# mLSTM gate preparation turned by VectorE and DMA, begun in the second token-major group; its loads and those of the heads two steps ahead of use

## The chip, the cores and the metric

The kernel runs on 1 core of one Trainium2 chip. The metric is the device time of one execution in microseconds. Before the change the median of 3 runs is 856.8 us (856.2 to 856.81).

## The reference

One encoder block on 512 tokens of width 1024. A normalised input is projected once into queries, keys, values and gates of three mixers; the mixers run beside each other; their outputs are gated, summed and projected; a convolutional gated FFN and a last norm follow. The part that matters here is the mLSTM mixer with its two directions, four heads of 128, and its gates:

```python
def rms_norm(x, g): ...
h = rms_norm(x, g)
proj = h @ w_in              # mLSTM q,k,v,o,gates | NA q,k,v | memory q | merge gates
i_fw, f_fw = gt[0] + b_ig[0], gt[1] + b_fg[0]     # the same for the backward direction
log_f = log_sigmoid(f_pre); a = cumsum(log_f) within a chunk; g = a[..., -1]
D = a[j] - a[s] + log_i[s]   (s <= j)
m_j = max(a + m_prev, max_s D)                    # stabiliser
P = exp(D - m_j) * (q k^T)
num = P v + exp(a + m_prev - m_j) * C_prev q      # state C of earlier chunks
h = num / max(|den|, exp(-m_j))
```

The result is normalised per head, multiplied by sigmoid(o) and merged with neighbourhood attention (8 heads) and attention into 256 memory tokens (4 heads).

## The kernel before, in words

**Matmuls.** All matrices are fp32. Each operand is split into a high and a low part, and one product is three matmuls of the reduced type (`mm3`, L359 to L362). The weights come as blocks by DMA on SP's queue (`wr`, L239); ACT makes the high part (L326), DVE the low part (L327), ahead of use, in two halves for the blocks of this stretch. TensorE (PE) is handed its work by this stream for the whole program.

**The stretch of the change.** After q and k of the mLSTM come three *token-major* groups (L637): widths 272, 512 and 256 of the projection, with tokens on the partitions. Group 0 gives the 16 gate pre-activations `Gt` (L653) and half of the values `va`; group 1 the other half and the first half of the neighbourhood values; group 2 the rest. The neighbourhood values go through a scratch tile `nv` (ACT L615, DVE L617) to the array `nav_d` in memory by a DMA on POOL's queue (L619). Between them the eight tiles of x are loaded again (`xn_load`, L628, SP), scaled by DVE (L632), copied by ACT (L633) and split (L634) into NH and NL for the projections that follow: `xaq` (four blocks, the memory queries), `o` (four blocks), `memk`/`memv` (8 half blocks), then the neighbourhood projections.

**Scratch.** `scr()` takes one of seven buffers of 128x512 in turn (pool `sp`). x tiles, `nv`, the tiles that `turn_out` writes, and `lr`, `mr` and `rr` of the preparation all come from it. A new tile waits until the last reader of the buffer's old content is done; for `nv` that is its DMA.

**The mLSTM stream.** `ml_all` is a generator. It is started behind the token-major groups and advanced by `step()` calls between the blocks of the main stream, RB = 1.3 of its yields per block, and at each it issues a part of the work: first `ml_prep` with 4 yields, then heads 0 to 3, where the parts of head h + 1 (`begin`, `middle`, `rest`, `last`) are interleaved with the four value blocks of head h. `ml_prep` turns the gates so that the four heads lie on partitions and the 512 tokens along the row: log-sigmoid on DVE (L680 to L700), layout `lfc` by POOL (L705, L706), four PE transposes into a PSUM bank (L709), four scans on DVE of the shapes 4x512 (L715, L716 for the stabiliser, L724, L725 for the cumulated sums), `rr` = difference to memory as `rd` (L734, L736, POOL), the chunk ends spread into `dg` (L743), and back again by four more PE transposes (L751) and a matmul with ones (L753). A head then uses `R`, a row of `rd` loaded to all partitions (L778), its masked copy (L781) and `K`, the turned keys (L179).

**turn_out / turn_in** (L166, L177) exist already for keys: DVE transposes 32x32 blocks (L170), four SP DMAs write the tile to memory in the block order (L173), and a later SP DMA reads it back (L179).

What sets the order: the code is issued in program order with a scheduler that orders each engine's instructions by when their data come; each engine runs its own list in order, so an instruction that waits holds up everything behind it on that engine.

Of the kernel before, what the change touches and what calls it, by code (L numbers as in the profile page):

```python
# [11 lines left out]
F32 = mybir.dt.float32  # L12
# [5 lines left out]
P = 128  # L18
# [112 lines left out]
def hybrid_block(ctx, tc, xT, memT, wflat, vecs, gbias, nabias, out):  # L131
# [501 lines left out]
        A.activation(NH[k], xs[k], AF.Copy)  # L633
        V.tensor_tensor(NL[k], xs[k], NH[k].bitcast(F32), op=ALU.subtract)  # L634

    xn_load()
    for c, n in enumerate(TMW):  # L637
        pss = [(mmps if c % 2 else atps)() for _ in range(NT)]
        g = 2 if n == 512 else 4
        for h in range(KT // g):  # L640
            ws = weights(("tm", c, h))
            if len(xs) < KT:
                xn_load()
            xn_part(2 * c + h if c < 2 else 6 + h)
            for t in range(NT):
                tsl = slice(t * P, (t + 1) * P)
                for k in range(g):
                    kk = g * h + k
                    mm3(pss[t][:, :n], XH[kk][:, tsl], XL[kk][:, tsl], ws[k][0], ws[k][1], kk == 0, kk == KT - 1)
        for t in range(NT):  # L650
            ps = pss[t]
            if c == 0:
                V.scalar_tensor_tensor(Gt[:, t, :], ps[:, :16], rc[:, t:t + 1], gb, op0=ALU.mult, op1=ALU.add)  # L653
                to_va(0, t, ps[:, 16:272])
            elif c == 1:
                to_va(1, t, ps[:, :256])
                to_nav(0, t, ps[:, 256:])
            else:
                to_nav(1, t, ps[:, :256])
    nav_v = nav_d.rearrange("(a r w) f -> a r w f", a=2, r=4)  # L660

    def load_vwin(hp):
# [13 lines left out]
    def ml_prep(load_R):  # L676
        gv = Gt.rearrange("p t (d k h) -> p t d k h", d=2, k=2)
        T4 = lambda a: a.rearrange("p (t d h) -> p t d h", t=4, d=2)
        f = tiny(32)
        V.tensor_copy(T4(f), gv[:, :, :, 1, :])  # L680
        af = tiny(32)
        V.scalar_tensor_tensor(af, f, -1.0, f, op0=ALU.mult, op1=ALU.max)
        e = tiny(32)
        A.activation(e, af, AF.Exp, scale=-1.0)
        r = tiny(32)
        V.tensor_scalar(r, e, 2.0, None, op0=ALU.add)
        V.reciprocal(r, r)
# [12 lines left out]
        V.scalar_tensor_tensor(lf, p, -2.0, mn, op0=ALU.mult, op1=ALU.add)  # L700
        yield
        lfc = cp.tile([P, NT, 100], F32, name="lfc")
# [5 lines left out]
        for t in range(NT):  # L708
            PE.transpose(pl[:100, t * P:(t + 1) * P], lfc[:, t, :], ident)  # L709
# [5 lines left out]
        V.tensor_tensor_scan(mr[0:4, :], lr[0:4, :], pl[64:68, :], NEG, op0=ALU.add, op1=ALU.max)  # L715
# [18 lines left out]
        V.tensor_tensor(rr[:36], cu[:36], mr[:36], op=ALU.subtract)  # L734
        for d in range(2):
            G.dma_start(rd[d], rr[32 * d:32 * d + 4, :])  # L736
        ml["rd"] = rd
        for d in range(2):
            for u in range(2):
                g = 2 * u + d  # L740
                gs = slice(32 * g, 32 * g + 4)
                ends = mr[gs].rearrange("p (t c) -> p t c", t=NT)[:, :, P - 1 if d == 0 else 0:][:, :, 0:1]
                V.tensor_tensor(dg[gs, g], ends.to_broadcast([4, NT, 4]),  # L743
                                ident[gs, gs].unsqueeze(1).to_broadcast([4, NT, 4]), op=ALU.mult)
# [5 lines left out]
        for t in range(NT):  # L750
            PE.transpose(pmv[:, t, :], mr[:100, t * P:(t + 1) * P], ident[:100, :100])  # L751
        pt = atps()
        PE.matmul(pt[:, :64], ones[:100], dg[:100].rearrange("p g t h -> p (g t h)"), start=True, stop=True)  # L753
        em = cp.tile([P, NT, 36], F32, name="em")
        A.activation(em, pmv[:, :, 0:36], AF.Exp, scale=-1.0)
        en = cp.tile([P, 2, 2, NT, 4], F32, name="en")
        V.tensor_copy(en, pt[:, :64].rearrange("p (u d t h) -> p u d t h", u=2, d=2, t=NT))
        mb = en[:, 0]
        bi = cp.tile([P, 2, NT, 4], F32, name="bi")
        V.tensor_tensor(en[:, 1], en[:, 1], mb, op=ALU.subtract)  # L760
        pr = (slice(1, 4), slice(0, 3)), (slice(0, 3), slice(1, 4))
        for d in range(2):
            V.tensor_tensor(bi[:, d], gv[:, :, d, 0, :], pmv[:, :, 64 + 32 * d:68 + 32 * d], op=ALU.subtract)
            V.tensor_tensor(ex[:, 0, d], bi[:, d], en[:, 1, d], op=ALU.add)
            J, Jp = pr[d]
            V.tensor_tensor(ex[:, 1, d, J], en[:, 1, d, J], mb[:, d, Jp], op=ALU.add)
        A.activation(ex, ex, AF.Exp)
        ml.update(em=em, bi=bi, mb=mb, ex=ex)
        yield

    def ml_all():

        def load_R(h):
            rd = ml["rd"]
            R, rm = [], []
            for d in range(2):
                t = tp.tile([P, S], F32, tag="R", name=nm("R"), bufs=4)
                SY.dma_start(t, rd[d, h].partition_broadcast(P))  # L778
                R.append(t)
                t = tp.tile([P, S], F32, tag="R", name=nm("R"), bufs=4)  # L780
                V.tensor_tensor(t.rearrange("p (j c) -> p j c", j=4), R[d].rearrange("p (j c) -> p j c", j=4),  # L781
                                msk[d].unsqueeze(1).to_broadcast([P, 4, P]), op=ALU.add)
                rm.append(t)
            return R, rm
# [64 lines left out]
        def values_J(h, J, E, Q, C, H, ss):  # L849
# [11 lines left out]
            emv = em[:, J, :].rearrange("p (a b) -> p a b", b=4)  # L861
            V.tensor_tensor(den, den, emv[:, 0:9:8, h], op=ALU.max)
# [28 lines left out]

        def begin(h):
            kt, C = own(h)
            st_[h] = dict(kt=kt, C=C, kq=keys(h, kt), R=ml.pop("R"))
# [10 lines left out]
        def last(h):  # L905
            x = st_[h]
            x["Q"] = [queries(h, d, x["R"][0]) for d in range(2)]
            if h < 3:
                ml["R"] = load_R(h + 1)
                ml["K"] = turn_in(kd[h + 1], "nab", 2)  # L910

        begin(0)
        yield
# [271 lines left out]
    yml = []  # L1185
    so = []
    gens.append(ml_all())

    xq = unit()
    for f in range(4):  # L1190
# [433 lines left out]
```

## Time and profile before

| | |
|---|---|
| median of 3 runs | 856.8 us (856.2 to 856.81) |
| profiled execution, its own time | 857.18 us |
| its span, first to last instruction | 855.4 us, mean granted clock 0.998 |
| busy: PE, DVE, ACT, POOL | 847.4, 603.4, 455.2, 150.8 us |
| mean DMA rate | 156 GB/s |
| L709 and L751 on PE | 4 instructions of 272 ns, 4 of 248 ns mean |
| token-major groups 0, 1, 2 | about 47 to 62, 62 to 84, 84 to 95 us |
| xaq blocks | begin near 95.4, 100.9, 106.7, 112.3 us |

How to read it: busy time of PE is close to the whole span, and a matmul's record is longer (0.39 us for 128x512) than the distance to the next one (0.23), since matmuls overlap in the pipeline; what one costs is read from that distance. The times of an engine's rows are the starts and durations, a bracket gives the idle time ahead of it and what ended it.

### The profile page before, as it was taken

Reading aid. Unit: us, or ns where it says so; the run is one execution under the profiler, and the core shown is the slowest. Engines: PE = TensorE matmul, PEld = TensorE weight load, DVE = VectorE, ACT = ScalarE, POOL = GpSimd, SP = SyncE. Lnnn points to the kernel's source line nnn. Section 1 sums busy time; section 2 is a strip of 40 time slices with the busy share of each in tenths; the row PEclk is TensorE's granted clock in tenths of the full one; section 3 lists DMA queues with packets and bytes.
Section 4 is the critical chain, followed back from the end, with each engine's and each line's share of the span. In section 5 each row is a group of like instructions: output and inputs, shape, how many; then the busy total and the mean of one; then the engine's idle time right before and its main releaser. Section 6 shows DMA issues by size and latency. Waiting matters only on the chain.

```text
span 855.4 us, 12106 instructions
## 1 busy us (share of the span) xinstructions
PE 847.4 (99%) x4010; PEld 711.8 (83%) x4010; DVE 603.4 (71%) x1194; ACT 455.2 (53%) x956; POOL 150.8 (18%) x236
## 2 busy tenths in 40 slices
PE   9999999999999999999999999999999999999997
PEld 7898988888888888888888888888888888888886
DVE  7699677865458658998586547767766677766773
ACT  7465557775446648887644334434444444533442
POOL 2000100000102830554000211211111111210211
PEclk9999999999999999999999999999999999999999
DMA  8236736563335846788523442544422223845842
GB/s 273 87 113 212 235 113 201 179 208 105 120 122 170 225 142 203 227 228 236 177 96 110 148 160 88 163 156 148 147 99 99 95 93 113 236 119 148 247 107 98
DMA packets 78158, 133.63 MB, mean 156 GB/s; under 512 B 10888, under 2 KB 38024, under 8 KB 78096
## 3 DMA queue, kind: packets, MB, share of 16 engines
q1 hardware_dynamic: 68144, 122.22, 44.2%
q0 software_dynamic: 9664, 10.51, 6.2%
q8 instruction: 31, 0.51, 0.2%
q14 instruction: 31, 0.25, 0.1%
q10 hardware_dynamic: 288, 0.14, 0.1%
HBM read 117.21 MB, written 15.62 MB: 155 GB/s over the span
## 4 chain that ended last, share of the span: by engine, by line
PE 98%; DMA 1%; issue 0%; ACT 0%; SPq 0%; DVE 0%; POOLq 0%; POOL 0%; ACTq 0%
PE mm L361 28%; PE mm L360 28%; PE mm L362 28%; PE at L360 3%; PE at L361 3%; PE at L362 3%; PE at L1023 1%; PE at L856 1%; PE at L858 1%; PE at L840 1%; DMA wr<-wflat 1%; PE at L990 0%; PE at L989 0%; PE at L800 0%; PE mm L542 0%
## 5 line engine op out<-in xcount | busy, mean ns | idle before, releaser
L360 PE MATMUL mm<-u,w 128*128 128x512 f32 x859 | 336.3, 391 | 0.0
L362 PE MATMUL mm<-u,w 128*128 128x512 f32 x859 | 335.0, 390 | 0.0
L361 PE MATMUL mm<-u,w 128*128 128x512 f32 x859 | 334.9, 390 | 0.0
L326 ACT ACTIVATE w<-wr 128x512 fp32r<-128x512 f32 (+1 forms) x256 | 159.6, 627 | 134.7 <-PE mm L362 96.9
L327 DVE TENSOR_TENSOR w<-wr,w 128x512 fp32r<-128x512 f32 (+2 forms) x257 | 177.7, 695 | 69.3 <-ACT w L326 67.1
L362 PEld LDWEIGHTS mm<-u,w 128*128 128x128 f32 x859 | 161.3, 188 | 33.9 <-DVE w L327 0.3
L360 PEld LDWEIGHTS mm<-u,w 128*128 128x128 f32 x859 | 161.5, 188 | 32.5
L361 PEld LDWEIGHTS mm<-u,w 128*128 128x128 f32 x859 | 161.5, 188 | 32.1
L669 POOL DMA_DIRECT2D u<-nav_d x128 | 62.0, 497 | 102.6 <-PE at L1023 51.7
L1344 POOL TENSOR_TENSOR s<-s,rb 128x512 f32<-128x512 f32 x21 | 36.3, 1728 | 180.3 <-DVE s L1342 180.3
L360 PE MATMUL mm<-w,u 128*128 128x512 f32 x160 | 62.8, 393 | 0.0
L362 PE MATMUL mm<-w,u 128*128 128x512 f32 x160 | 62.4, 390 | 0.0
L361 PE MATMUL mm<-w,u 128*128 128x512 f32 x160 | 62.4, 390 | 0.0
L263 ACT ACTIVATE w<-u 128x512 fp32r<-128x512 f32 x48 | 30.1, 630 | 53.5 <-PE mm L362 39.3
L263 DVE TENSOR_TENSOR w<-u,w 128x512 fp32r<-128x512 f32 x48 | 33.1, 690 | 29.4 <-ACT w L263 29.0
L362 PEld LDWEIGHTS mm<-w,u 128*128 128x128 f32 x160 | 30.1, 188 | 6.3
L360 PEld LDWEIGHTS mm<-w,u 128*128 128x128 f32 x160 | 30.1, 188 | 6.0
L361 PEld LDWEIGHTS mm<-w,u 128*128 128x128 f32 x160 | 30.1, 188 | 6.0
L562 ACT ACTIVATE s<-pad,vec 128x512 f32<-128x512 f32 x30 | 24.4, 812 | 8.1 <-DVE pad L560 7.3
L366 ACT ACTIVATE u<-s 128x512 fp32r<-128x512 f32 x14 | 8.9, 632 | 36.1 <-DVE s L1352 36.1
L1313 POOL TENSOR_TENSOR acc<-acc,s 128x512 f32<-128x512 f32 x7 | 9.1, 1295 | 93.2 <-ACT s L1312 93.2
L563 DVE SCALAR_TENSOR_TENSOR s<-pad,vec,s 128x512 f32<-128x512 f32 x30 | 22.5, 749 | 3.7 <-ACT s L562 3.7
(308 smaller groups left out, 1176.7 us busy)
## 6 DMA issues: line engine op xcount, KB each, us to landing
wr<-wflat SPq DMA_DIRECT2D x124, 512.0 KB, 3.5
u<-wflat SPq DMA_DIRECT2D x48, 256.0 KB, 5.2
td<-s SPq DMA_DIRECT2D x172, 64.0 KB, 1.8
U<-td SPq DMA_DIRECT2D x41, 256.0 KB, 3.7
s<-xT SPq DMA_DIRECT2D x24, 256.0 KB, 4.1
nab<-nabias SPq DMA_DIRECT2D x16, 256.0 KB, 3.9
u<-nav_d POOLq DMA_DIRECT2D x128, 32.0 KB, 3.6
u<-wflat POOLq DMA_DIRECT2D x16, 256.0 KB, 7.4
```

Of the source, the lines that this page charges most:

```text
L263: chain[eng] = getattr({"V": V, "A": A, "G": G}[eng], what)(*a, **k).ins
L326: A.activation(h[:, u:v], src, AF.Copy)
L327: V.tensor_tensor(l[:, u:v], src, h[:, u:v].bitcast(F32), op=ALU.subtract)
L360: PE.matmul(ps, lh, rh, start=start, stop=False)
L361: PE.matmul(ps, lh, rl, start=False, stop=False)
L362: st["mm"] = PE.matmul(ps, ll, rh, start=False, stop=stop).ins
L366: A.activation(h, src, AF.Copy, scale=scale)
L562: A.activation(t1, pad[:, 0:512], AF.Identity, scale=vcol(w, i), bias=vcol(b, i))
L563: V.scalar_tensor_tensor(t1, pad[:, 1:513], vcol(w, n + i), t1, op0=ALU.mult, op1=ALU.add)
L669: G.dma_start(vw[r * 32:(r + 1) * 32, i * 256:(i + 1) * 256], nav_v[hf, r, CW[b]:CW[b] + 32, hp * 256:(hp + 1) * 256])
L1313: G.tensor_tensor(acc2, acc2, sq, op=ALU.add)
L1344: chain["G"] = G.tensor_tensor(c, c, rb2, op=ALU.mult).ins
```

## The change

`turn_out` and `turn_in` take the place of the eight PE transposes. `lfc` is widened to 128 columns, written to memory (`ld`) and read back as `lt`; ACT copies two parts of it into `lr` and `gr`; the scans read those from scratch tiles instead of PSUM. Likewise `mr` is written out after the scans (`md`) and read back as `mt`, from which `em` and `bi` are made. The preparation has 8 yields in place of 4. The code of the token-major groups moves behind the line that starts the generator, and five steps are called there: two in the second group, two in the third, one behind it. `load_R` only loads; `masked` adds the masks in `middle`; the load of the next head's K moves from `last` to `middle`.

```diff
-    xn_load()
-    for c, n in enumerate(TMW):
...
+        lfc = cp.tile([P, NT, P], F32, name="lfc")
...
-        pl = atps()
-        for t in range(NT):
-            PE.transpose(pl[:100, t * P:(t + 1) * P], lfc[:, t, :], ident)
-        lr = scr()
-        A.activation(lr[:36], pl[:36, :], AF.Copy)
-
+        ld = turn_out(lfc)
         mr = scr()
-        G.memset(mr[:100], 0.0)
-        V.tensor_tensor_scan(mr[0:4, :], lr[0:4, :], pl[64:68, :], NEG, op0=ALU.add, op1=ALU.max)
-        V.tensor_tensor_scan(mr[32:36, ::-1], lr[32:36, ::-1], pl[96:100, ::-1], NEG, op0=ALU.add, op1=ALU.max)
+        G.memset(mr, 0.0)
...
+        yield
+        lt = turn_in(ld, "K", 1)
+        yield
+        lr, gr = scr(), scr()
+        for x, o in ((lr, 0), (gr, 64)):
+            A.activation(by4(x[:36]).rearrange("p s (i a) -> p s i a", i=4), lt[o:o + 36], AF.Copy)
+        V.tensor_tensor_scan(mr[0:4, :], lr[0:4, :], gr[0:4, :], NEG, op0=ALU.add, op1=ALU.max)
+        V.tensor_tensor_scan(mr[32:36, ::-1], lr[32:36, ::-1], gr[32:36, ::-1], NEG, op0=ALU.add, op1=ALU.max)
...
+        md = turn_out(by4(mr))
...
+        mt = turn_in(md, "K", 1).rearrange("p s i a -> p i s a")
+        ml["K"] = turn_in(kd[0], "nab", 2)
         ml["R"] = load_R(0)
-        ml["K"] = turn_in(kd[0], "nab", 2)
-        pm = atps()
-        pmv = pm[:, :400].rearrange("p (t c) -> p t c", t=NT)
-        for t in range(NT):
-            PE.transpose(pmv[:, t, :], mr[:100, t * P:(t + 1) * P], ident[:100, :100])
+        yield
+        yield
...
+        def masked(R):
...
             x = st_[h]
             states(h, x["kt"], x["C"])
+            x["R"] = masked(ml.pop("R"))
+            if h < 3:
+                ml["K"] = turn_in(kd[h + 1], "nab", 2)
...
     gens.append(ml_all())
+
+    xn_load()
+    for c, n in enumerate(TMW):
...
+                    mm3(pss[t][:, :n], XH[kk][:, tsl], XL[kk][:, tsl], ws[k][0], ws[k][1], kk == 0, kk == KT - 1)
+                    if (c == 2 or c == 1 and h > 1) and t == 1 and k == 1:
+                        step(1)
...
+    step(1)
```

Lines shift with the edit: in the changed kernel L730 is the matmul of L753, L701, L697, L698, L702 are the four scans (L724, L715, L716, L725), L712 is L734, L721 is L743, L755 is L778. L170, L173, L179, L327, L617, L628, L632 and L634 keep their numbers.

The first place is DVE between the last x tile and the weight halves of the second `xaq` block. Buffer numbers tell the tiles apart: `s_145` is the last x tile before, `w_155` and `w_156` are the halves; `s_157`, `w_174` and `w_175` are the same in the changed kernel. Before:

```order
L632 SCALAR_TENSOR_TENSOR s_145_954<-s_145_954,vec_79,rb_x_446 128x512
L634 TENSOR_TENSOR u_100_629<-s_133_889,u_98_627 128x512
L327 TENSOR_TENSOR w_147_1009<-wr_130_881,w_147_1009 128x512
L327 TENSOR_TENSOR w_148_1012<-wr_130_881,w_148_1012 128x512
L634 TENSOR_TENSOR u_100_629<-s_145_954,u_98_627 128x512
L617 SCALAR_TENSOR_TENSOR nv_149_1066<-at_138_942,rc_x_393,nv_149_1066 128x128 x2
L617 SCALAR_TENSOR_TENSOR nv_150_1071<-at_139_943,rc_x_393,nv_150_1071 128x128 x2
L617 SCALAR_TENSOR_TENSOR nv_151_1076<-at_140_944,rc_x_393,nv_151_1076 128x128 x2
L327 TENSOR_TENSOR w_155_1089<-wr_142_946,w_155_1089 128x512
L617 SCALAR_TENSOR_TENSOR nv_152_1081<-at_141_945,rc_x_393,nv_152_1081 128x128 x2
L327 TENSOR_TENSOR w_156_1092<-wr_142_946,w_156_1092 128x512
```

In the changed kernel, from the last x tile on, to the first half and the transpose:

```order
L632 SCALAR_TENSOR_TENSOR s_157_999<-s_157_999,vec_79,rb_x_446 128x512
L634 TENSOR_TENSOR u_100_629<-s_157_999,u_98_627 128x512
L701 SCALAR_TENSOR_TENSOR cu_164_1089<-on_145_947,s_162_1083 4x512
L697 SCALAR_TENSOR_TENSOR s_144_945<-s_162_1083,s_163_1084 4x512
L698 SCALAR_TENSOR_TENSOR s_144_945<-s_162_1083,s_163_1084 4x512
L702 SCALAR_TENSOR_TENSOR cu_164_1089<-on_145_947,s_162_1083 4x512
L721 TENSOR_TENSOR dg_1153<-s_144_945,ident_120 4x16 x2
L327 TENSOR_TENSOR w_174_1167<-wr_154_991,w_174_1167 128x512
L170 STREAM_TRANSPOSE s_165_1094<-s_144_945 128x4x4x32
```

Behind these come, in this order, four pairs of L617, then:

```order
L617 SCALAR_TENSOR_TENSOR nv_170_1146<-at_153_990,rc_x_393,nv_170_1146 128x128 x2
L712 TENSOR_TENSOR s_171_1151<-cu_164_1089,s_144_945 36x512
L721 TENSOR_TENSOR dg_1153<-s_144_945,ident_120 4x16 x2
L327 TENSOR_TENSOR w_175_1170<-wr_154_991,w_175_1170 128x512
L327 TENSOR_TENSOR w_184_1219<-wr_159_1054,w_184_1219 128x512
```

The scans, the dg copies, the transpose and L712 now stand between the last x tile and the two halves, which stood behind L634 with only L617 between.

The second place is SP's queue around the last x tile. Before, its load stands behind a weight block and ahead of two more; the names in brackets are the semaphores it waits for, DMASW those of transfers issued by POOL:

```order
L239 DMA wr_130_881<-wflat 128x1024 [waits DMAHW4_49,DVE_49]
L628 DMA s_133_889<-xT 128x512 [waits DMAHW5_49,DVE_49]
L239 DMA wr_142_946<-wflat 128x1024 [waits DMAHW6_49,DVE_49,Activation_49]
L628 DMA s_145_954<-xT 128x512 [waits DMAHW7_49,Activation_49]
L239 DMA wr_146_1007<-wflat 128x1024 [waits DMAHW2_49,DMAHW0_49,DVE_49]
```

In the changed kernel:

```order
L173 DMA td_143_940<-s_142_938 32x4x128 [waits DMAHW2_49]
L239 DMA wr_159_1054<-wflat 128x1024 [waits DMAHW3_49,DVE_49]
L628 DMA s_157_999<-xT 128x512 [waits DMAHW4_49,DMASW0_49]
L179 DMA U_158_1022<-td_143_940 128x512 [waits DMAHW5_49,DMAHW2_49,DMAHW7_49,DMAHW1_49,DMAHW0_49]
L239 DMA wr_173_1165<-wflat 128x1024 [waits DMAHW6_49,DVE_49]
```

The load of the last x tile now stands behind four scatters and a weight block more, and it waits for a transfer of POOL: the first store of nav_d, whose scratch buffer it takes.

The third place is PE, where the second group of transposes stood. Before:

```order
L362 MATMUL mm_1292<-u_626,w_1229 128x512
L751 MATMUL at_1312<-ident,s_1214 128x100 x4
L753 MATMUL at_1317<-dg,ones 128x64
L360 MATMUL mm_1292<-u_626,w_1229 128x512
L361 MATMUL mm_1292<-u_628,w_1229 128x512
```

In the changed kernel:

```order
L362 MATMUL mm_1269<-u_626,w_1219 128x512
L730 MATMUL at_1279<-dg,ones 128x64
L360 MATMUL mm_1269<-u_626,w_1219 128x512
L361 MATMUL mm_1269<-u_628,w_1219 128x512
L362 MATMUL mm_1269<-u_626,w_1219 128x512
```

Only the matmul with ones is left, in the third `xaq` block instead of the fourth; the four of L709 are gone in the same way.

More of the change, by code (lines that the diff above doesn't have):

```diff
@@ L634, in xn_part @@
         V.tensor_tensor(NL[k], xs[k], NH[k].bitcast(F32), op=ALU.subtract)
-    xn_load()
-    for c, n in enumerate(TMW):
[L638 to L644, printed above, removed]
-            for t in range(NT):
[L646 to L649, printed above, removed]
-        for t in range(NT):
[L651 to L659, printed above, removed]
     nav_v = nav_d.rearrange("(a r w) f -> a r w f", a=2, r=4)
@@ L779, in load_R @@
                 R.append(t)
+            return R
+        def masked(R):
+            rm = []
+            for d in range(2):
                 t = tp.tile([P, S], F32, tag="R", name=nm("R"), bufs=4)
@@ L860, in values_J @@
             A.activation(den, pv[:, :, 128], AF.Abs)
-            emv = em[:, J, :].rearrange("p (a b) -> p a b", b=4)
-            V.tensor_tensor(den, den, emv[:, 0:9:8, h], op=ALU.max)
+            V.tensor_tensor(den, den, em[:, :, J, h], op=ALU.max)
             V.reciprocal(den, den)
@@ L893, in begin @@
             kt, C = own(h)
-            st_[h] = dict(kt=kt, C=C, kq=keys(h, kt), R=ml.pop("R"))
+            st_[h] = dict(kt=kt, C=C, kq=keys(h, kt))
         def middle(h):
@@ L1187, in hybrid_block @@
     gens.append(ml_all())
+    xn_load()
+    for c, n in enumerate(TMW):
+        pss = [(mmps if c % 2 else atps)() for _ in range(NT)]
+        g = 2 if n == 512 else 4
+        for h in range(KT // g):
+            ws = weights(("tm", c, h))
+            if len(xs) < KT:
+                xn_load()
+            xn_part(2 * c + h if c < 2 else 6 + h)
+            for t in range(NT):
+                tsl = slice(t * P, (t + 1) * P)
+                for k in range(g):
+                    kk = g * h + k
+                    mm3(pss[t][:, :n], XH[kk][:, tsl], XL[kk][:, tsl], ws[k][0], ws[k][1], kk == 0, kk == KT - 1)
+                    if (c == 2 or c == 1 and h > 1) and t == 1 and k == 1:
+                        step(1)
+        for t in range(NT):
+            ps = pss[t]
+            if c == 0:
+                V.scalar_tensor_tensor(Gt[:, t, :], ps[:, :16], rc[:, t:t + 1], gb, op0=ALU.mult, op1=ALU.add)
+                to_va(0, t, ps[:, 16:272])
+            elif c == 1:
+                to_va(1, t, ps[:, :256])
+                to_nav(0, t, ps[:, 256:])
+            else:
+                to_nav(1, t, ps[:, :256])
+    step(1)
     xq = unit()
```

12 lines of the change are left out of this document (4 added, 8 removed).

## The prediction, on record before the changed kernel ran

> **What bounds the kernel now.** I read the page's busy times first, then the waits of PE, then the busy times by stretch.
>
> ```profile
> PE   9999999999999999999999999999999999999997
> PE at L394 <- DVE warm L388: 1.2, 1, 1.2
> PE at L1023 <- PE at L990: 0.4, 1, 0.4
> PE mm L542 <- ACT w L326: 0.2, 1, 0.2
> 73.00:89.00 16.00, 16.00 (x92) 14.10 (x92) 14.56 (x28) 9.87 (x21) 3.37 (x6) 1.00 0.79 267
> 89.00:97.00 8.00, 8.00 (x62) 7.74 (x62) 6.03 (x15) 4.99 (x10) 1.59 (x3) 1.00 0.84 254
> 97.00:103.00 6.00, 6.00 (x28) 4.95 (x28) 2.67 (x6) 3.17 (x7) 1.06 (x2) 1.00 0.71 222
> 103.00:124.00 21.00, 21.00 (x103) 17.53 (x102) 14.02 (x33) 11.45 (x26) 1.04 (x2) 1.00 0.42 123
> ```
>
> PE is busy in every slice but the last, and its list of waits is whole in three rows: the warm-up before the inputs are there, 0.4 us late in the neighbourhood attention, 0.2 us at the start. In the stretches the change touches (start and end, length, then busy PE, weight load, DVE, ACT, POOL, granted clock, DMA share, GB/s) PE is full at a granted clock of 1.00. So the rule for the sum is simple: a matmul taken off PE is worth its time; work added on DVE, ACT, POOL or the queues costs nothing until a weight half or an operand comes too late, and from there PE's wait goes onto the end microsecond by microsecond. DVE is the engine to watch: 14.56 of 16 us at 73 to 89.
>
> **The transposes taken from PE.** These are a gain on the bounding engine.
>
> ```profile
> 106.11 0.39 PE L362 MATMUL mm<-u,w 128*128 128x512 f32 x1
> 106.34 0.60 PE L709 MATMUL at<-ident,lfc 128*100 128x128 f32 x4
> 106.69 0.48 PE L360 MATMUL mm<-u,w 128*128 128x512 f32 x1
> 107.01 0.39 PE L361 MATMUL mm<-u,w 128*128 128x512 f32 x1
> 114.29 0.51 PE L751 MATMUL at<-ident,s 100*128 100x100 f32 x4
> 114.69 0.41 PE L753 MATMUL at<-dg,ones 100*128 100x64 f32 x2
> ```
>
> Without L709 its successor L360 would issue at 106.34 and L361 one step of 0.23 later, at 106.57, where it issues at 107.01: 0.44 us. The four of L751 hold PE from 114.29 to 114.69, 0.40 us, and the matmul behind them (L753) stays. Sum **-0.84 us**, 0.1% of the span, and all that comes off PE: the rest of the diff removes no matmul.
>
> **What is added beside PE.** Two DVE transposes, ten SP transfers (two scatters of four, two loads) and one more ACT copy replace the eight PE transposes.
>
> ```profile
> 61.27 0.70 DVE L170 STREAM_TRANSPOSE s<-u 128x512 f32<-128x512 f32 x1
> 61.89 0.71 DVE L563 SCALAR_TENSOR_TENSOR s<-pad,vec,s 128x512 f32<-128x512 f32 x1
> 83.90 0.33 SPq L628 DMA_DIRECT2D s<-xT  x1
> ```
>
> DVE's next instruction starts 0.62 after a transpose: 1.2 us of DVE for two; ten SP issues at 0.33 are 3.3 us of its queue. By their sum they cost nothing: DVE is idle for 2 us of 89 to 97 and 3.3 of 97 to 103, ACT for 3 of each. What they cost depends on where they stand, so I followed the queue.
>
> **The wait that the order makes.** The scratch pool has seven buffers, and the preparation now takes several of them (the turned tiles, two copies, the result) while the last tiles of x are still to come. The last one, s_157, gets the buffer of the first store to nav_d, and its load waits until that store has landed. Before, the last load (the SP row above) was issued at 83.90 without that wait.
>
> ```profile
> 82.91 0.75 DVE L632 SCALAR_TENSOR_TENSOR s<-s,vec,rb_x 128x512 f32<-128x512 f32 x1
> 83.57 0.86 DVE L617 SCALAR_TENSOR_TENSOR nv<-mm,rc_x,nv 128x128 fp32r<-128x128 f32 x3
> 85.28 1.38 DVE L617 SCALAR_TENSOR_TENSOR nv<-mm,rc_x,nv 128x128 fp32r<-128x128 f32 x5
> 86.18 1.60 POOL L619 DMA_DIRECT2D nav_d<-nv  x3 [0.64 <-DVE nv L617]
> DMA to landing us min/median/max: 2.5/3.2/5.6
> DMA to landing us min/median/max: 3.3/3.6/5.2
> ```
>
> The two last rows are the landings of L619 (nav_d) and of L628 (xT), each minimum, median, maximum. Now the steps. DVE is in the same order up to 82.91. Behind it the changed order puts a transpose, a weight half and L634, three instructions of about 0.6, before L617: its first pair ends near 83.57 + 1.8 + 0.6 = 86.0. POOL issues a store some 0.55 after its pair (the second pair of before ended with the first of the five of 85.28, near 85.63, and its store went out at 86.18), so near 86.6. It lands 2.5 to 5.6 later, by the median at 89.8; the load of x goes out, and lands 3.3 to 5.2 later. Early end 86.6 + 2.5 + 3.4 = 92.5; median 86.6 + 3.2 + 3.7 = 93.5; both at their maxima 97.5.
>
> DVE is in order, and everything behind L632 on s_157 waits with it: L634, four scans, the first half of the weights of the second xa query block (w_174), the transpose, eight L617, L712, and the second half, w_175. Their prices:
>
> ```profile
> 87.77 1.41 DVE L632 SCALAR_TENSOR_TENSOR s<-s,vec,rb_x 128x512 f32<-128x512 f32 x2
> 89.22 0.69 DVE L634 TENSOR_TENSOR u<-s,u 128x512 fp32r<-128x512 f32 x1
> 89.83 1.40 DVE L327 TENSOR_TENSOR w<-wr,w 128x512 fp32r<-128x512 f32 x2
> 107.70 1.21 DVE L715 TENSOR_TENSOR_SCAN s<-s,at 4x512 f32<-4x512 f32 x1 [1.87 <-issue]
> 112.63 0.69 DVE L327 TENSOR_TENSOR w<-wr,w 128x512 fp32r<-128x512 f32 x1
> 113.24 0.68 DVE L734 TENSOR_TENSOR s<-cu,s 36x512 f32<-36x512 f32 x1
> 113.84 0.70 DVE L743 TENSOR_TENSOR dg<-s,ident 4x16 f32<-4x16 f32 x4
> 114.57 1.29 DVE L327 TENSOR_TENSOR w<-wr,w 128x512 fp32r<-128x512 f32 x2
> 101.35 0.39 PE L362 MATMUL mm<-u,w 128*128 128x512 f32 x1
> 104.07 0.39 PE L362 MATMUL mm<-u,w 128*128 128x512 f32 x1
> 95.57 0.69 DVE L327 TENSOR_TENSOR w<-wr,w 128x512 fp32r<-128x512 f32 x1 [0.27 <-ACT w L326]
> 96.70 0.68 DVE L327 TENSOR_TENSOR w<-wr,w 128x512 fp32r<-128x512 f32 x1
> ```
>
> L632, the ACT copy between and L634 go from 87.77 to 89.83, 2.06. The scans run 107.70 to 112.63, 4.93. Two dg copies are half of 114.57 - 113.84, 0.36. The first half: 0.61. Then transpose 0.61, eight L617 at 0.26 (86.57 - 85.28 for five) 2.06, L712 0.60, two dg 0.36, the second half 0.69. To the end of w_174: 7.96 behind x's landing. To the end of w_175: 12.28, and about 0.25 until PE has loaded it, an estimate. PE wants the low parts at 101.35 and 104.07. So w_175 stalls PE unless x has landed by 104.07 - 12.53 = **91.5**; w_174 unless it has by 101.35 - 8.21 = 93.1. With x at 92.5, 93.5, 97.5 the whole stall is 1.0, 2.0, 6.0. Before, the same two halves were done at 96.26 and 97.38 and nothing was near. In that crowded stretch (DMA share 0.84 at 89 to 97, and the new scatters with it) I lean to x later than the median, 93.9: a stall of **+2.4 us**, 0.8 of it at the first half. The POOL and SP rows are those of the old order, so this term may lie between nothing (x before 91.5) and 6.0.
>
> The Trainium skill, page "DMA: Bandwidth & Descriptors", section "Issuing engines are not separate DMA queues", says that transfers issued by different engines share the 16 DMA engines and interleave. The DMA share rows agree, and by it the store from POOL and the loads from SP slow each other; with x at its longest landing behind a median store (95.0) the stall would be 3.5 us.
>
> **What moves later.** The head preparation stands one generator step further on: keys, states and values come about 15 matmuls earlier, their masks and K loads with other heads. The waits that this can relieve are DVE's, not PE's:
>
> ```profile
> 123.92 0.69 DVE L781 TENSOR_TENSOR R<-R,msk 128x512 f32<-128x512 f32 x1 [3.61 <-DMA R<-rd]
> 127.55 0.65 DVE L327 TENSOR_TENSOR w<-wr,w 128x512 fp32r<-128x512 f32 x1
> rd<-s POOLq DMA_DIRECT2D x2, 8.0 KB, 5.4
> ```
>
> DVE sits 3.61 us for a row of R, and the weight half that stands behind it is done at 128.20, shortly before PE uses it; moving it gains no PE time, as PE waits nowhere there. What could be late next is R: its rd store takes 5.4 to land, and the pushed-back L712 starts it. I put +0.3 for that (0 to 1). Sum: 857.18 (the profiled execution; span 855.4) - 0.84 + 2.4 + 0.3 = 859.0. The median of three runs lies 0.38 below that execution, so the forecast is **858.7 us**, +0.2%.
>
> **Rivals.**
> *Hidden (not slower).* The store lands fast and x by 91.5. For it: the old loads of x landed in 3.3 at best, and DVE might pass L617 earlier. Against: it needs the two in 4.9 us from 86.6, below their two minima, 5.8. The time: -0.84, 855.96 to 857 while the stall is under 1 us; the point from which it turns is a stall of 0.84, x at 92.3.
> *Further stalls.* The delay spreads to the R loads, the memory-token loads and the halves of 128 to 160, where a half ended at 128.20. For it: with x at 93.9 the two halves end at 101.9 and 106.2, 5.6 and 8.8 later than before, and all of DVE behind them with it. Against: DVE's 3.3 us of idle in 97 to 103, and more up to 124 (14.02 busy of 21), make most of it up. Two more waits of 1 to 1.5 on top: 860 to 862.
> *The clock falls.* A stall of PE could cost clock. The last window, where PE ends, is the only one under 1.00. If 7 us of matmuls ran at half rate, +3.5: about 862. The Trainium skill, page "TensorE: Matmul & The Clock Gate", section "Part 1: The HAM clock gate", has the clock halved only after about 3.4 us of idle; stalls of 0.8 and 1.6 would not reach it, a stall of 6 us would; no row here shows PE idle that long in mid-run.
> *The step moves nothing.* That the order is not as told is excluded by the order of the instructions itself; what is not seen is when each wait ends.
>
> **How the numbers follow.** A measurement of this kernel tells about 0.2%, 1.7 us. The stall near 2.4 us has a chance of 0.57, and its own range is 857.0 to 859.7 (stalls of 1.0 to 3.4). Hidden has 0.23; further stalls 0.15; clock 0.05. Faster by 0.2% means under 855.1, below -0.84 for which no row is at hand: 0.06, out of hidden. Same (855.1 to 858.5) takes the rest of hidden, 0.17, and half of the stall's, 0.28: 0.45. Slower: 0.29 + 0.15 + 0.05 = 0.49. The range reaches from 855.4 to the 6.0 us stall and what follows, 862.2.
>
> **What would show it.** Right: PE waits at the second xa query block (101 to 106 us) for DVE L327, SP's last xT load issued near 89.5 behind a POOL store, DVE idle before L632 until it lands; no L709 and L751 on PE. Wrong: PE's list of waits as short as before (hidden); the wait at another weight half, near 128 or 150 (further stalls); a granted clock under 1.00 in 100 to 110 (clock); or a stall longer than 6 us.

## The result, and the profile after

The changed kernel takes 862.18 us (median of 4 runs, 861.36 to 862.91) against 856.8 before: ratio 1.0064, 95% interval 1.0051 to 1.0077. It is 5.4 us slower, where 1.9 was forecast. The profiled execution is 862.91 us with a span of 861.1.

The waits of PE in the changed kernel (line waited at, what ended the wait; total, number, longest):

```profile
PE mm L362 <- DVE w L327: 3.5, 2, 3.2
PE at L394 <- DVE warm L388: 1.2, 1, 1.2
PE mm L360 <- ACT w L326: 0.2, 1, 0.2
```

The first row is new, and it stands where it was expected. PE's own rows show the place, and something more:

```profile
101.11 0.39 PE L361 MATMUL mm<-u,w 128*128 128x512 f32 x1
104.73 0.79 PE L362 MATMUL mm<-u,w 128*128 128x512 f32 x1 [3.23 <-DVE w L327]
105.32 0.63 PE L360 MATMUL mm<-u,w 128*128 128x512 f32 x1
105.75 0.63 PE L361 MATMUL mm<-u,w 128*128 128x512 f32 x1
...
107.45 0.46 PE L362 MATMUL mm<-u,w 128*128 128x512 f32 x1
...
109.08 0.50 PE L362 MATMUL mm<-u,w 128*128 128x512 f32 x1
...
133.50 0.39 PE L362 MATMUL mm<-u,w 128*128 128x512 f32 x1
134.13 0.50 PE L360 MATMUL mm<-u,w 128*128 128x512 f32 x1 [0.24 <-ACT w L326]
...
135.09 0.50 PE L362 MATMUL mm<-u,w 128*128 128x512 f32 x1 [0.23 <-DVE w L327]
```

A matmul of this size starts 0.23 us after the one before it. The third of the second `xaq` block starts 3.62 after: 3.39 lost. Then the starts are 0.59 and 0.43 apart until 107.45, not 0.23: the clock has been halved (granted clock 0.54 from 104 to 106 us), and 1.36 is lost over six starts. At the second weight half (109.08) 0.3 goes, near 126 and 127 us 0.6, near 134 and 135 1.0, near 300 0.3. That is 7.0. The absent transposes give 0.84 back, and two short waits of the execution before (0.6 near 382, 0.16 near 300) are not there. What is left, 5.4, is the distance between the last matmuls of the two traces (848.93 and 854.32).

DVE's rows show what is late (a bracket gives the idle time and what ended it), with SP's and POOL's issues:

```profile
86.57 2.35 POOL L619 DMA_DIRECT2D nav_d<-nv  x4 [8.69 <-DVE nv L617]
89.08 0.35 SPq L628 DMA_DIRECT2D s<-xT  x1
91.01 0.69 DVE L327 TENSOR_TENSOR w<-wr,w 128x512 fp32r<-128x512 f32 x1
96.82 0.75 DVE L632 SCALAR_TENSOR_TENSOR s<-s,vec,rb_x 128x512 f32<-128x512 f32 x1 [5.12 <-DMA s<-xT]
98.88 1.21 DVE L701 TENSOR_TENSOR_SCAN cu<-on,s 4x512 f32<-4x512 f32 x1
103.98 0.69 DVE L327 TENSOR_TENSOR w<-wr,w 128x512 fp32r<-128x512 f32 x1
105.22 2.12 DVE L617 SCALAR_TENSOR_TENSOR nv<-at,rc_x,nv 128x128 fp32r<-128x128 f32 x8
107.25 0.67 DVE L712 TENSOR_TENSOR s<-cu,s 36x512 f32<-36x512 f32 x1
108.34 1.89 DVE L327 TENSOR_TENSOR w<-wr,w 128x512 fp32r<-128x512 f32 x3
```

The landing of the eight loads of x in the changed kernel:

```profile
DMA to landing us min/median/max: 2.7/6.6/7.7
```

The store goes out at 86.57, the load of the last x tile at 89.08, and it lands 7.7 us later (the maximum; before it was 5.2). DVE waits 5.12 us for it and ends the first weight half at 104.67. From 98.88 on its rows show no idle time, and the second half, the first of the three at 108.34, is done at 109.03. PE at full clock would have come to that half near 107.6, by its starts of 0.23, and would have waited there. So the slow clock cost nothing of its own here: the 5.05 us lost up to 109.08 (3.39, 1.36 and 0.3) are what the late x tile costs by way of DVE's list.

### The profile page after: what moved, and what is told of

Same layout as the page of the kernel before. It is cut to its first block, busy times and chain, and to the rows that moved or that the text cites. A ratio compares the mean times of both kernels' runs of the same rounds, so it can differ in the third digit from the quotient of the medians.

```text
span 861.1 us, 12115 instructions
## 1 busy us (share of the span) xinstructions
PE 849.5 (99%) x4002; PEld 711.1 (83%) x4002; DVE 601.1 (70%) x1196; ACT 456.8 (53%) x957; POOL 150.1 (17%) x236
## 4 chain that ended last, share of the span: by engine, by line
PE 91%; DMA 4%; DVE 3%; issue 1%; ACT 1%; SPq 0%; POOLq 0%; POOL 0%; ACTq 0%; DVEq 0%
PE mm L362 26%; PE mm L360 26%; PE mm L361 26%; PE at L361 3%; PE at L360 3%; PE at L362 3%; DMA s<-xT 2%; DMA s<-memT 2%; PE at L1006 1%; PE at L838 1%; PE at L840 1%; DVE w L327 1%; PE at L822 1%; DMA wr<-wflat 0%; PE at L973 0%
## 5 line engine op out<-in xcount | busy, mean ns | idle before, releaser
L362 PE MATMUL mm<-u,w 128*128 128x512 f32 x859 | 335.7, 391 | 3.5 <-DVE w L327 3.5
L360 PE MATMUL mm<-u,w 128*128 128x512 f32 x859 | 336.5, 392 | 0.3 <-ACT w L326 0.2
L326 ACT ACTIVATE w<-wr 128x512 fp32r<-128x512 f32 (+1 forms) x256 | 159.5, 628 | 141.3 <-PE mm L362 100.0
L327 DVE TENSOR_TENSOR w<-wr,w 128x512 fp32r<-128x512 f32 (+2 forms) x257 | 175.1, 686 | 78.5 <-ACT w L326 76.8
L362 PEld LDWEIGHTS mm<-u,w 128*128 128x128 f32 x859 | 161.6, 188 | 39.5 <-DVE w L327 5.6
L360 PEld LDWEIGHTS mm<-u,w 128*128 128x128 f32 x859 | 161.7, 188 | 33.7 <-ACT w L326 1.6
L360 PE MATMUL mm<-w,u 128*128 128x512 f32 x160 | 62.7, 392 | 0.0
L362 PE MATMUL mm<-w,u 128*128 128x512 f32 x160 | 62.3, 389 | 0.0
L362 PEld LDWEIGHTS mm<-w,u 128*128 128x128 f32 x160 | 30.0, 188 | 6.3
L360 PEld LDWEIGHTS mm<-w,u 128*128 128x128 f32 x160 | 30.1, 188 | 6.1
L562 ACT ACTIVATE s<-pad,vec 128x512 f32<-128x512 f32 x30 | 24.4, 812 | 11.2 <-DVE pad L560 10.5
L366 ACT ACTIVATE u<-s 128x512 fp32r<-128x512 f32 x14 | 8.9, 632 | 36.1 <-DVE s L1363 36.1
```

The source lines that it names most:

```text
L326: A.activation(h[:, u:v], src, AF.Copy)
L327: V.tensor_tensor(l[:, u:v], src, h[:, u:v].bitcast(F32), op=ALU.subtract)
L360: PE.matmul(ps, lh, rh, start=start, stop=False)
L362: st["mm"] = PE.matmul(ps, ll, rh, start=False, stop=stop).ins
L366: A.activation(h, src, AF.Copy, scale=scale)
L562: A.activation(t1, pad[:, 0:512], AF.Identity, scale=vcol(w, i), bias=vcol(b, i))
```

## The experiments

Each ran beside the kernel before on one chip; ratios are to that.

**1. x early.** One more load of x where the last but one is made, so that the last tile takes its buffer ahead of the preparation.

```diff
             if len(xs) < KT:
                 xn_load()
+                if c == 1 and h == 3:
+                    xn_load()
```

> The changed kernel, with the load of the last x tile issued one block earlier (with the one before it), so that it takes its scratch buffer ahead of the preparation and waits for no store. Late x (my theory): the load goes out near 84, lands before 89, and the 3.4 us wait of PE at the first half of the second xaq block, the slow clock behind it (1.4) and the waits near 126 and 134 (1.6) go; a wait of up to 1.2 can stay there, since the turned gates now land last; time 856.0 to 857.8. Placement (rival): the four scans and what stands around them between x and the weights are enough for the stall: a wait over 2 us stays at the same place, time 859 to 862. Further stalls (rival): the waits near 126 and 134 come from the moved head and memory loads themselves: they stay, with 1 us or more, and the time is 857.5 to 859.

Measured 861.95 us, ratio 1.0058 (1.0045 to 1.0070): as slow as the change. PE's rows:

```profile
117.17 0.50 PE L362 MATMUL mm<-u,w 128*128 128x512 f32 x1 [0.72 <-DVE w L327]
...
119.36 0.40 PE L362 MATMUL mm<-u,w 128*128 128x512 f32 x1
121.41 0.50 PE L360 MATMUL mm<-u,w 128*128 128x512 f32 x1 [1.65 <-ACT w L326]
...
122.61 0.50 PE L362 MATMUL mm<-u,w 128*128 128x512 f32 x1 [0.47 <-DVE w L327]
```

The wait at 101 and the slow clock are gone, as I expected: late x did make that wait. But 4.7 us are now lost between 116 and 144, and no theory had that size. So late x is enough for the first wait and is not what the time hangs on.

**2. Begin in the third group.** No steps in the second token-major group.

```diff
-                    if (c == 2 or c == 1 and h > 1) and t == 1 and k == 1:
+                    if c == 2 and t == 1 and k == 1:
```

> The changed kernel, with the steps of the second token-major group left out: the preparation is turned in the same way by VectorE and DMA, but begins in the third group, three steps run there in place of five. The last x tile is then loaded as before the change, with no wait for a store. Late x: no wait of PE over 1 us in 95 to 110 us, time 856.0 to 857.5. Placement: the scans, wherever they stand ahead of weight halves, cost a stall: over 859. Further stalls: waits of PE near 120 to 140 stay: 857.5 to 859.

Measured 857.96 us, ratio 1.0011 (1.0002 to 1.0019), with a wait of 0.5 us left near 127 and one of 0.3 near 301. The same turn by VectorE and DMA, begun two steps later, costs a fifth of it: the place decides. Here x is early and the scans stand behind the value copies (they start at 102.69, the copies at 92.38), so this run does not part the two.

**3. Stores twice.**

```diff
...
+        if c == 0 and t > 0:
+            G.dma_start(nav_x[t * P:(t + 1) * P, :], nv)
```

> The changed kernel with three of the four first stores from POOL written a second time, to memory that nothing reads: 768 KB more in the DMA engines' queues ahead of the last x tile, nothing else. If x landed late because bytes queue ahead of it (280 GB/s in that stretch), it lands 2.7 us later than 96.7, and the wait of PE at the second xaq block grows from 3.4 to about 6: time near 865. If its 7.7 us are the latency of one transfer whatever stands ahead, x still lands at 96.7 and the time stays near 862.

One run, 863.22 us. x was issued 0.95 later, at 90.03 (its store landed later), and took 7.97 us; the wait grew from 3.23 to 3.8. Two of the three extra stores went out ahead of it, and its own landing took only 0.3 longer. So 512 KB more on POOL's queue added little here, in one execution, and neither expectation fits in full.

**4. The heads' loads alone**, in the kernel before.

```diff
...
+            x["R"] = masked(ml.pop("R"))
+            if h < 3:
+                ml["K"] = turn_in(kd[h + 1], "nab", 2)
...
-                ml["K"] = turn_in(kd[h + 1], "nab", 2)
```

> The kernel before, with one part of the change alone: masks added in the head's middle part, the K of the next head loaded there too. PE waits nowhere that these could relieve, so by every theory but one the time is that of before, 856.8 within 0.2%. By further stalls, if the moved loads themselves make weight halves late, PE waits of 0.5 us or more appear between 120 and 220 us and the time is 857.5 or more.

Measured 856.81 us, ratio 1.0 (0.9991 to 1.0009); PE waits for nothing but its warm-up. This part is free, and brings nothing.

**5 and 6. R later**, on top of 2 and of 1.

```diff
-        ml["R"] = load_R(0)
         yield
         yield
+        ml["R"] = load_R(0)
```

> As the run that begins in the third group, with the first loads of R issued two yields later, behind two memory-token loads and a weight block on SP's queue. Blocked queue (my second theory): R's loads stand at the head of SP's queue until the rd stores have landed, and the memory-token tiles, the K tile and weight blocks behind them come late; then the one wait left, near 127 us, goes, and the time is 856.0 to 857.3, 0.7 to 1.5 under 857.96. Bytes (rival): the loads and stores themselves fill the DMA engines at that time whatever their order; the wait stays within 0.3 and the time near 858.

> As the run with the last x tile loaded one block earlier, with the first loads of R issued two yields later, behind a memory-token load and a weight block. Blocked queue: of the 4.7 us that PE lost at 116 to 144 in that run most goes, PE's waits there fall under 1.5 us, time 857 to 859. Bytes: the four stores of the third group's values, which stood together at 103 to 105 behind the scans and took 5.5 to 6.7 us to land, with weights and tokens among them, are what makes all of these late; the waits stay over 3 us, time 860.5 to 862.5.

On top of 2: 857.41 us, ratio 1.0006 (0.9997 to 1.0015), and the wait near 127 is gone; the time cannot be told from that of run 2. On top of 1: 860.35 us, ratio 1.0038 (1.0025 to 1.0052), 1.5 less than run 1 when each is taken against its own kernel before. The trace of run 6 is that of its slowest execution (862.41) and has waits of 1.6 and 1.9 us. R's loads still went out at 113.15 only, when the rd store had landed, ahead of the K tile, memory tokens and weights; so the second run took the block away in part, and its number lies between the two theories and hardly clear of noise from run 1.

**7. The price on PE.** Each group of four transposes five times over, in the kernel before.

```diff
-        for t in range(NT):
-            PE.transpose(pl[:100, t * P:(t + 1) * P], lfc[:, t, :], ident)
+        for _ in range(5):
+            for t in range(NT):
+                PE.transpose(pl[:100, t * P:(t + 1) * P], lfc[:, t, :], ident)
...
```

> The kernel before, with each of the two groups of four PE transposes issued five times over. By my price of 0.84 us for the two groups, four more of each add 3.4 us less the slower first matmul, which is paid once: 32 more transposes at 0.08 to 0.11 us each, 2.6 to 3.5 us; time 859.4 to 860.3. If PE's transposes cost nothing (covered by something else) the time stays at 856.8.

Measured 860.26 us against 856.71, ratio 1.0037 (1.0023 to 1.0050). In its trace (L710, L753 and L755 are L709, L751 and L753 of the kernel before):

```profile
106.70 2.35 PE L710 MATMUL at<-ident,lfc 128*100 128x128 f32 x20
108.81 0.48 PE L360 MATMUL mm<-u,w 128*128 128x512 f32 x1
116.40 1.88 PE L753 MATMUL at<-ident,s 100*128 100x100 f32 x20
118.12 0.36 PE L755 MATMUL at<-dg,ones 100*128 100x64 f32 x2
```

Twenty take 2.11 and 1.72 us from start to the next start; four took 0.35 and 0.40, so sixteen more of each cost 3.1. The term of the transposes was right.

**8. Scans behind the value copies.** x early as in 1, and the two steps of the third group put behind it.

```diff
-                    if (c == 2 or c == 1 and h > 1) and t == 1 and k == 1:
+                    if c == 1 and h > 1 and t == 1 and k == 1:
                         step(1)
...
-    step(1)
+    step(2)
```

> As the run with the last x tile loaded one block earlier, with the two steps in the third token-major group put behind it, so that its value copies and their four stores go out ahead of the scans (near 92 to 97, as before the change). Bunching (my third theory): in that run PE lost 4.7 us at 116 to 144 because the scans held the value copies until 102 to 104, so that four stores, the rd stores, memory tokens and weights came together at 103 to 113; now they are apart, PE's waits between 100 and 145 fall under 1 us and the time to 856 to 858. Blocked queue: R's loads behind the rd stores are the cause by themselves; waits of over 2 us stay, 859 or more.

Measured 857.08 us, ratio 1.0004 (0.9995 to 1.0014): 4.9 less than 1. PE waits nowhere between 60 and 299 us. First rows of run 1, then rows of this run (L714 is the rd store, L755 R's load, L763 its mask, L589 a load of memory tokens, L239 one of a weight block):

```profile
94.47 1.21 DVE L701 TENSOR_TENSOR_SCAN cu<-on,s 4x512 f32<-4x512 f32 x1 [2.07 <-ACT s L696]
101.91 2.15 DVE L617 SCALAR_TENSOR_TENSOR nv<-at,rc_x,nv 128x128 fp32r<-128x128 f32 x8
103.04 2.10 POOL L619 DMA_DIRECT2D nav_d<-nv  x4 [11.39 <-DVE nv L617]
105.13 1.04 POOL L714 DMA_DIRECT2D rd<-s  x2
111.78 0.80 SPq L755 DMA_DIRECT2D R<-rd  x2
112.63 0.43 SPq L589 DMA_DIRECT2D s<-memT  x1
115.82 0.69 DVE L763 TENSOR_TENSOR R<-R,msk 128x512 f32<-128x512 f32 x1 [2.82 <-DMA R<-rd]
117.14 0.33 SPq L239 DMA_DIRECT2D wr<-wflat  x1
```

```profile
97.34 1.20 DVE L701 TENSOR_TENSOR_SCAN cu<-on,s 4x512 f32<-4x512 f32 x1
97.95 0.53 POOL L619 DMA_DIRECT2D nav_d<-nv  x1 [0.95 <-ACT s L696]
106.35 1.06 POOL L714 DMA_DIRECT2D rd<-s  x2 [7.87 <-DVE s L712]
106.17 0.44 SPq L589 DMA_DIRECT2D s<-memT  x1
110.36 0.89 SPq L755 DMA_DIRECT2D R<-rd  x2
112.25 1.22 SPq L239 DMA_DIRECT2D wr<-wflat  x1
```

In run 1 the scans wait for the turned gates and hold DVE to 99.2; the eight copies and their four stores come at 102 to 105, on the heels of them the rd stores, which land 6.3 to 6.6 us later. R's loads stand on SP until 111.78, and the second memory-token load (112.63) and a weight block (117.14) behind them; on DVE a mask waits 2.82 us for R in front of the weight half that PE wants at 117, and the weight block's load goes out only when that half is done (117.11). In run 8 the last value store goes out at 97.95, the rd stores land in 4.0 us though they are issued later, and the same two loads go out at 106.17 and 112.25, 6.5 and 4.9 us earlier.

**9. x ahead of the weights** on SP's queue; x still waits for the store.

```diff
+        if st.get("xl"):
+            with tc.issue_after(st.pop("xl")):
+                SY.dma_start(r[:, :n], src)
+            return
...
```

> The changed kernel, with the weight block (512 KB) that stood ahead of the last x tile on SP's queue issued behind it; x still waits for the store. If what is ahead on SP's own queue made x land in 7.7 us, it now lands in 3.5 to 5, at 93 to 94.5, and PE's first wait falls from 3.2 to 0.5 to 1.5 us with no slow clock behind it; what is behind may still come late, so the time is 857.5 to 861. If everything in flight shares the engines whatever its order, x lands after 7 us or more and the time stays near 862.

Measured 865.25 us, ratio 1.0088 (1.0072 to 1.0104). In the profiled execution 2.3 us went at the very start (PE at half clock up to 10.5 us), where the edit changes nothing, so its times stand 2.3 later than those of the change; whether its other executions lost this too is not shown, and its median says little of the edit. Two rows of DVE and PE, and PE's waits (line numbers here are higher: L366 is L362, L364 is L360, L330 and L331 are L326 and L327, L638 is L632):

```profile
96.38 0.75 DVE L638 SCALAR_TENSOR_TENSOR s<-s,vec,rb_x 128x512 f32<-128x512 f32 x1 [2.38 <-DMA s<-xT]
104.28 0.50 PE L366 MATMUL mm<-u,w 128*128 128x512 f32 x1 [0.49 <-DVE w L331]
```

```profile
PE mm L364 <- ACT w L330: 2.9, 1, 2.9
PE mm L366 <- DVE w L331: 2.1, 3, 1.5
```

The load of x lands in 4.2 us (92.07 to 96.28) instead of 7.7, and the first wait shrinks from 3.23 to 0.5 with no slow clock. So without the 512 KB ahead on SP's own queue most of the lateness is gone. But that block alone does not make x late: before the change a weight block was issued 0.83 us ahead of the same load too (83.07 and 83.90), no store of POOL's had gone out yet, and x landed in 3.3 us. So it is the block and the stores together, as far as these rows go; the load of U that follows x on the same queue (89.61 in the change, 92.60 here) was not tried apart. Nor is 7.7 a fixed price: run 11, with the same block and stores ahead, has 5.9. And again nothing is won by it: waits of 1.5 and 2.9 us come near 123 and 129, and the last matmul starts at 857.09, 2.8 us behind that of the change, 2.3 of it from the start.

**10. Scans behind the value copies, R later**: 8 with the edit of 5.

> As the run before the last, with R's first loads two yields later as well. If both the bunching and the blocked queue are gone, PE waits nowhere between 60 and 300 us, and the time is that of before less the transposes: 855.8 to 857. It is the candidate to beat the kernel before; by the rival (thin slack of the weight halves in other executions) it stays at 857 or over.

Measured 857.01 us, ratio 1.0 (0.9991 to 1.0009). The best of the runs with the turn, and no faster than before. PE's waits:

```profile
PE at L394 <- DVE warm L388: 1.2, 1, 1.2
PE mm L542 <- ACT w L326: 0.7, 1, 0.7
PE at L360 <- ACT U L1110: 0.5, 1, 0.5
```

The last is near 301 us, in the memory attention. From the same matmul near 25 us to the middle of the program (the 1690th of the 3381 wide matmuls) PE takes 437.2 us here and 437.5 in run 4, which has the transposes. Run 4 does not have this wait: about 0.8 us are lost again by it, for a turned tile that lands no earlier (ACT takes it at 300.34 here, at 300.12 in run 4). The rest is inside what single executions differ by at their start (0.2 to 1.0 us of wait at L542, where the first weights arrive).

**11. x late, scans behind**: the change with the edit of 8 alone.

> The changed kernel, with the two steps of the third token-major group put behind it, and the last x tile left as the change has it (its load waits for the store). With the run that has both x early and the steps behind (857.08), the one with x early alone (861.95) and the changed kernel (862.18), this fills the table of two by two. If the scans' place is what costs, and late x only delays what stands behind it: the first weight half of the second xaq block now stands ahead of the scans and is in time (near 99.5), the second comes behind them, near 105.1 against 104.1: one wait of PE of up to 1.3 us, no slow clock, time 857.3 to 859. If late x costs by itself, a wait of over 3 us stays near 101 and the time is over 860.

Measured 858.19 us, ratio 1.0018 (1.0009 to 1.0027). The second weight half is done at 103.8, a wait of 0.2 us, and two more of 0.7 come near 124 and 126. With 1, 8 and the change this gives, in us above the kernel before that ran beside each:

| | x late | x early |
|---|---|---|
| scans ahead of the value copies | 5.4 | 5.1 |
| scans behind them | 1.7 | 0.3 |

Down a column is 3.7 and 4.9 us, along a row 0.2 and 1.4. Each number is good to about 1 us, so the columns are clear of noise and the rows hardly. With x late the move also puts the first weight half ahead of the scans, and in that trace x landed at 94.6, 2.1 us earlier than in the change.

**12. The turn at the old place**, no steps in the groups.

```diff
-                    if (c == 2 or c == 1 and h > 1) and t == 1 and k == 1:
-                        step(1)
...
-    step(1)
```

> The changed kernel with no steps in the token-major groups: the preparation is turned by VectorE and DMA, and the heads' loads are moved, but all begins where it did before, and with four more yields of preparation the heads come three steps later than before. If the turn itself is harmless (no added wait of its own, 0.84 us less on PE), PE waits nowhere between 95 and 250 us and the time is 855.8 to 857.3. If the turn's transfers or the later heads make something late, a wait of over 1 us shows between 120 and 260 and the time is over 857.5.

Measured 863.65 us, ratio 1.0087 (1.0073 to 1.0100), slower than the change. DVE's rows, and PE's at the place:

```profile
146.88 0.69 DVE L763 TENSOR_TENSOR R<-R,msk 128x512 f32<-128x512 f32 x1 [1.57 <-DMA R<-rd]
147.49 0.42 DVE L1216 TENSOR_SCALAR u<-u 128x512 f32<-128x512 f32 x1
147.82 0.69 DVE L327 TENSOR_TENSOR w<-wr,w 128x512 fp32r<-128x512 f32 x1
```

```profile
148.56 0.50 PE L361 MATMUL mm<-w,u 128*128 128x512 f32 x1 [2.34 <-DVE w L327]
...
150.08 0.63 PE L360 MATMUL mm<-w,u 128*128 128x512 f32 x1
```

With eight yields and the old start the heads come three steps later; a mask then waits for R in front of a weight half, PE waits 2.3 us and falls to half clock. The wait and the slow starts cost 4.2 us; 1.2 go near 246 and 259, and 0.9 at the start of this execution. So at the old place the turned chain comes too late; how early it may begin, and in front of what, is where the change went wrong.

## Why the prediction was right and wrong

**What bounds it**: right. Every loss seen is a wait of PE or its clock, and their sum is the difference.

**The transposes, -0.84**: right in size (run 7), and of no use: even where every new wait ahead of 299 us is cleared (run 10), a wait near 301 us takes back most of it. I had written that a matmul taken off PE is worth its time; here it held only up to the next transfer that did not come earlier.

**The wait the order makes**: right in place, mechanism and steps. The store went out at 86.57 (86.6 forecast), the first half ended 7.94 us behind the arrival of x (96.73; 7.96 forecast), and PE waited at the low part of the first half. What failed is the size of the term +2.4: it measured 5.05. x landed at 96.7, not 93.9, though its load went out earlier than forecast (89.08): I took landings of before (3.3 to 5.2) for a load that goes out with a 512 KB block ahead of it on its own queue and three stores of POOL's not yet landed, and it took 7.65. The steps behind it were right: with x at 96.73 my own formula gives 96.73 + 12.53 - 104.07 = 5.2. The halves share it otherwise, 3.39 at the first, then 1.36 as slow starts and 0.3 at the second, because PE at half clock reaches the second one later.

The Trainium skill, page "DMA: Bandwidth & Descriptors", section "Issuing engines are not separate DMA queues", says that transfers of all engines interleave on the same 16 DMA engines. The landings agree in that POOL's stores and SP's block made x late together: 3.3 us with the block and no store ahead of it (before), 4.2 with three stores and no block (run 9), 7.65 with both. They were not alike byte for byte: 512 KB more from POOL's queue added 0.3 (run 3), 512 KB less ahead on SP's took 3.4 off (run 9).

**The clock**: I gave it 0.05, since I had split the stall in two short ones. It fell, and PE lost 1.36 us in slow starts, but at full clock it would have waited for the second half as long, so this added nothing to the time. The page "TensorE: Matmul & The Clock Gate" of the Trainium skill, section "Part 1: The HAM clock gate", puts the halving after about 3.4 us of idle. The 3.23 us here come near it; other runs show it sooner:

| PE's wait, us | run | half clock behind it |
|---|---|---|
| 1.5, 1.6, 1.65 | 9, 6, 1 | no |
| 1.87 | 6 | yes, 3.4 us long |
| 2.34 | 12 | yes |
| 2.9, 3.23, 3.8 | 9, the change, 3 | yes |

In run 6 the slow starts come 1.1 us after the wait's end:

```profile
137.99 0.49 PE L840 MATMUL at<-u,E 128*128 128x129 f32 x2 [1.87 <-DVE u L827]
138.31 1.06 PE L782 MATMUL at<-u,u 128*128 128x128 f32 x8
139.12 0.66 PE L360 MATMUL mm<-u,w 128*128 128x512 f32 x1
139.58 0.63 PE L361 MATMUL mm<-u,w 128*128 128x512 f32 x1
```

So in mid-run the measurements put the point, here, between 1.65 and 1.87 us of wait, with small matmuls beside it in run 6; at the program's start less was enough (0.64 us in run 9). Whether it also matters when a wait comes was not tried.

**What is late next, +0.3**: the other term that failed, and here the reason failed too. I had written that DVE's idle time in 97 to 124 would "make most of it up". It was 1.6 us near 126 to 135, and 0.3 near 300, where the kernel before has 0.16. I had counted DVE's idle time and not asked what those waiting instructions hold: the eight value copies behind the scans let go four stores of 256 KB together, just ahead of the rd stores and R's loads, with tokens and weights behind them on SP. With 5.05 in place of 2.4 and 1.9 in place of 0.3 the sum comes out at the 5.4 measured, once the two short waits of before (0.76) are taken off.

**The cause**: I named the late x tile. It makes the first wait, but taking it away alone gains 0.2 us (run 1), since then PE comes earlier to the halves at 116 to 124 and waits there. What decides is where the two steps with the scans stand: behind the value copies 3.7 to 4.9 us are gone (runs 11 and 8). The rival that I called further stalls had the mechanism; I had given it 0.15, as an addition to the first stall and not as what lies behind it.

**What stays open.** Between the bytes of the bunched stores and the hold that R's loads put on SP's queue runs 6 and 8 do not decide: run 6 took the hold away in part (1.5 us), run 8 changed both. Why runs 8 and 10, which show no new wait of PE ahead of 299 us, are not faster than before is shown to 0.9 and 0.8 us by the wait near 301; the rest is not shown. In run 5 that wait is 0.3 us, but its trace is of one of its fastest executions (856.75 against a median of 857.41); what the others wait for is not shown.

## What to carry to other kernels

Before moving work earlier on an engine that keeps its order, list what then stands behind it and what each of these lets go, stores and loads first: here the place of four scans ahead of eight short copies was worth 3.7 to 4.9 us. A wait removed shows its worth only when the next one is known: build the two by two of the suspected causes before naming one. And price a transfer's landing by what is under way when it goes out, on its own queue and on the others, not by the median of its kind: here 3.3 us became 7.7.

## What was not expected of the hardware

A wait of PE of 1.87 us in the midst of full work was followed by half clock for 3.4 us (granted clock 0.54 from 139.0 to 142.5 in run 6), while 1.65 us (run 1) was not. In run 6, where nothing behind it was late, this cost 1.6 us more than the wait itself: eight starts of 0.43 in place of 0.23.

The landing of the same 256 KB load took 3.3 us with a 512 KB block just ahead on its queue and no store gone out yet (before), 4.2 with three stores of 256 KB and no block (run 9), and 5.9 and 7.7 with both (run 11 and the change).
